# Turning k, q, v and the delta output by VectorE blocks and transfers instead of TensorE transposes

## The chip, the cores and the metric

The kernel runs on one core of a Trainium2 chip. The metric is the time of one execution on the device, in microseconds (us); the time of a kernel is the median of its runs. A core has TensorE (PE, matmuls; PEld is its loading of weights), VectorE (DVE), ScalarE (ACT), GpSimd (POOL) and SyncE (SP), which work side by side, each through its own instructions in order. SP and POOL, and now and then ACT, issue the transfers (DMAs) between DRAM and the core's memory.

## The reference, cut to what matters

One layer of a decoder with 512 new tokens of a prompt (`x_prompt`) and 8 single tokens (`x_sample`). All data are float32.

```python
xn = rmsnorm(h, norm_mix)
proj = xn @ w_in                        # 2048 -> q | k | v | z (1024 each) | beta, decay (8 each) | pool (1024)
qkv_c, new_conv = short_conv(conv_buf, proj[..., :3072], conv_w)    # 4 taps over the tokens, then SiLU
q = l2norm(q) * (128 ** -0.5); k = l2norm(k)                        # 8 heads of 128
# per chunk of tokens, with the cumulated gates g and beta b:
m  = strictly_lower(b * (k @ k.T) * decay)        # then (I + m) is inverted
qk = lower((q @ k.T) * decay)
v_new = u - w @ S
o  = (q * exp(g)) @ S + qk @ v_new
S  = S * exp(g_last) + (k * exp(g_last - g)).T @ v_new
dn_out = rmsnorm(o, dn_norm) * silu(z)
h = h + concat(dn_out, pool_out) @ w_out
h = h + swiglu(rmsnorm(h, norm_ffn)); y = rmsnorm(h, norm_final)
```

## The kernel before, in words

Activations lie with their features on the 128 partitions and the 520 tokens (8 samples, 512 of the prompt) along the row. A projection tile of 128 columns is a `product`: 16 steps over the input features, each with three matmuls (high and low parts of both operands) for each of two halves of the tokens (`CHUNKS`). The weights come in granules of 128 x 1024: SP loads `raw` (L131), ScalarE rounds it to `hi` (L135), VectorE takes the rest as `lo` (L137), with three buffers of each.

The changed part runs from 40 to about 520 us. For each half of the heads (`b` = 0, 1; four heads) it does the four k tiles, then the four z tiles, then for each head a q tile and a v tile. `qkv_tile` ends with the four taps on VectorE (L737, L739) and SiLU on ScalarE (L740).

The smaller work of the delta rule is written as Python generators which `Weave` steps through: `product` calls `weave.step()` after each of its steps (16 times a product), and a task's `yield n` says how many steps it rests. There are two tracks, and each runs its tasks in the order in which they were added, a task not before its delay. TensorE's instructions run in just this order of the program. For the other engines and the DMA queues a planner (the Tile framework) orders the instructions by priority and by when it expects them to be ready; each engine then takes its own list in order. Loads and cuts of weights, and evictions, have a raised priority.

The tasks:
- `keys(h)`: K times K per chunk of 128 tokens (L766), the transposes of k's tile (L769), the sums of squares of the transposed tile by ScalarE (`squares`, L757), the factors `sck` on POOL and VectorE, `nn` (K times K with its factors and decay, L781) and `kd` (k with tokens on partitions, times a factor, L783). The diagonal 32 x 32 blocks of `nn` go to DRAM (`nd_d`, L788).
- `eliminate(b)`: inverts all the diagonal blocks of four heads on VectorE (L807, L809), and sends the results to DRAM (`ud_d`, L810, L813), from where `qv_tiles` loads them into `utf` (L1093).
- `delta(h, qT, vT)`: `nn` with the inverse blocks (L831), the transposes of q (L838) and their squares, three rounds (`it`) that widen the inverse (L850 on TensorE, L852 on VectorE), with K times Q (L857) and `aq` (L860) in the first and the transposes of v (L865) and `vs` (L867) in the second, then four chunks of the recurrence (L877 to L896) with R, W and S passing between TensorE, VectorE and ScalarE, and last the norm of the output (`on`, L910).
- `gate(h, on)`: 8 steps later, the transposes of `on` (L916), and one VectorE instruction that multiplies them into `mix[h]` (L918).

`d1tile(tag, ...)` gives a buffer of the pool by its tag, of which there are `BUFS[tag]`. `pst()` gives one of five PSUM banks. Later stages (w_out, the gate and up projections, the down projection) are Strassen products with the queue of POOL carrying the intermediate (`a_d`, `st`, L1776).

Of the kernel before, what the change touches and what calls it, by code (L numbers as in the profile page):

```python
# [8 lines left out]
F32 = mybir.dt.float32  # L9
# [3 lines left out]
ALU = mybir.AluOpType  # L13
# [22 lines left out]
    "ext": 2, "y": 1, "ys": 1, "g3": 3, "junk": 1, "ss": 2, "rr": 2, "nb": 1, "u": 1, "tm": 2, "xt_": 1, "uu": 2,  # L36
    "qts": 1, "fq": 2, "aq": 1, "vs": 1, "R": 2, "W": 2, "S": 2, "so": 2, "ro": 2, "s0": 2, "s2": 1, "kd": 4, "st": 2,
}
# [31 lines left out]
def decoder_kernel(ctx, tc, x_prompt, x_sample, state_delta, state_conv, state_pool, norm_mix, w_in,  # L70
# [450 lines left out]
    with ExitStack() as p1:  # L521
# [208 lines left out]
        def qkv_tile(sec, h, out, ext=None):  # L730
# [10 lines left out]
            pool.tensor_copy(ccp[:, :, t], ext[:, SEQ:SEQ + 3])  # L741

        def decay(h):

            gcb = d1tile("g3", [P, SEQ], "gcb")
            sp.dma_start(gcb, gcr_d[h:h + 1, :].broadcast_to([P, SEQ]))
            dm = d1tile("g3", [P, SEQ], "dm")
            for c in range(NCH):
                dve.scalar_tensor_tensor(dm[:, ck(c)], gcb[:, ck(c)], gcs[:, c, h:h + 1], mneg,
                                         op0=ALU.subtract, op1=ALU.min)  # L750
            act.activation(dm, dm, AF.Exp)
            return gcb, dm
# [7 lines left out]
        def keys(h):  # L760
            kT, nn = mixb[:, h % 4, 0:SEQ], mixb[:, 4 + h % 4, 0:SEQ]
            kd = kds[h] = d1tile("kd", [P, SEQ], "kd")
            _, dm = decay(h)
            gp_ = pst()
            for c in range(NCH):
                te.matmul(gp_[:, ck(c)], kT[:, ck(c)], kT[:, ck(c)], start=True, stop=True)  # L766
            ktp = pst()
            for c in range(NCH):
                te.transpose(ktp[:, ck(c)], kT[:, ck(c)], ident)  # L769
            ss = d1tile("ss", [P, NCH], "ss")  # L770
            squares(ktp, ss)
            dve.tensor_scalar(ss, ss, EPS, None, op0=ALU.add)
# [7 lines left out]
            for c in range(NCH):  # L780
                dve.scalar_tensor_tensor(nn[:, ck(c)], gp_[:, ck(c)], fk[:, c:c + 1], dm[:, ck(c)],  # L781
                                         op0=ALU.mult, op1=ALU.mult)
            dve.tensor_tensor(v3(kd), v3(ktp), bc3(ad), op=ALU.mult)  # L783
            yield 6 if h < 3 else 2
# [31 lines left out]

        def delta(h, qT, vT):
            kT, nn, kd = mixb[:, h % 4, 0:SEQ], mixb[:, 4 + h % 4, 0:SEQ], kds[h]
# [16 lines left out]
            pool.tensor_copy(v3(cur), udf)  # L835
            qtp = pst()
            for c in range(NCH):
                te.transpose(qtp[:, ck(c)], qT[:, ck(c)], ident)  # L838
            ss = d1tile("ss", [P, NCH], "ss")
            squares(qtp, ss)  # L840
            dve.tensor_scalar(ss, ss, EPS, None, op0=ALU.add)
            fq = d1tile("fq", [P, NCH], "fq")
            pow_mhalf(fq, ss)
            dve.tensor_scalar(fq, fq, float(P) ** -0.5, None, op0=ALU.mult)
            yield 2
            for it in range(3):
                yp = v3(pst())
                j = slice(32 * it + 32, P)
                for c in range(NCH):
# [3 lines left out]
                                         op0=ALU.mult, op1=ALU.add)  # L853
                if it == 0:
                    gq_ = pst()
                    for c in range(NCH):
                        te.matmul(gq_[:, ck(c)], kT[:, ck(c)], qT[:, ck(c)], start=True, stop=True)  # L857
                    aq = d1tile("aq", [P, SEQ], "aq")
                    for c in range(NCH):
                        dve.scalar_tensor_tensor(aq[:, ck(c)], gq_[:, ck(c)], fk[:, c:c + 1], dm[:, ck(c)],  # L860
                                                 op0=ALU.mult, op1=ALU.mult)
                if it == 1:
                    vtp = pst()
                    for c in range(NCH):
                        te.transpose(vtp[:, ck(c)], vT[:, ck(c)], ident)  # L865
                    vs = d1tile("vs", [P, SEQ], "vs")
                    dve.tensor_tensor(v3(vs), v3(vtp), bc3(ik), op=ALU.mult)  # L867
                yield 2
# [3 lines left out]
            for c in range(NCH):  # L872
# [24 lines left out]
                S = S2  # L897
                yield 1
            sp.dma_start(nd_prompt[0, 0, h], S)

# [9 lines left out]
            dve.tensor_tensor(v3(on), v3(op_), bc3(ro), op=ALU.mult)  # L910
            weave.add(gate(h, on), 1, 8)

        def gate(h, on):
            otp = pst()
            for c in range(NCH):
                te.transpose(otp[:, ck(c)], on[:, ck(c)], ident)  # L916
            yield 1
            dve.scalar_tensor_tensor(mix[h][:, NB:NTOK], otp, dnw, mix[h][:, NB:NTOK], op0=ALU.mult, op1=ALU.mult)  # L918

# [169 lines left out]
        def qv_tiles(h):  # L1089
            utf = utfs[h % 2].rearrange("p a c j -> p (a c) j")  # L1090
            for q in range(4):
                r = slice(32 * q, 32 * q + 32)
                sp.dma_start(utf[r, :, r], ud_d[h, q].rearrange("a c s j -> s (a c) j"))  # L1093
            qT = d1tile("s0", [P, SEQ], "qT")
            qkv_tile(0, h, qT)
            vT = d1tile("s2", [P, SEQ], "vT")
            qkv_tile(2, h, vT)
            weave.add(delta(h, qT, vT), 0, 1)

        kds = {}  # L1100
        for b in range(2):
            for h in range(4 * b, 4 * b + 4):
                qkv_tile(1, h, mixb[:, h % 4, 0:SEQ],
                         {0: ext_first, 1: ext_second}.get(h))
                if h == 0:
                    weave.add(states())
                    weave.add(gates(), 1)
                weave.add(keys(h), 1, 16)
            weave.add(eliminate(b), 1)
# [967 lines left out]
```

## Time and profile before

| | |
|---|---|
| median of 3 runs | 2161.36 us (2161.24 to 2161.99) |
| span of the profiled execution | 2158.9 us |
| TensorE busy | 2136.1 us |
| VectorE busy | 1746.4 us |
| ScalarE busy | 929.6 us |
| POOL busy | 433.8 us |
| moved by DMA | 297.04 MB |

The times given are those of the unprofiled runs. The profiled execution has a span from its first to its last instruction; that is shorter than a run's time by what lies around it (2161.36 - 2158.9 = 2.5 us here).

How such lines are read: a group reads "line engine operation out<-in shape xcount | busy us, mean ns of one | idle before us <-who ended it". A line of a timeline reads "start us, us, engine line operation out<-in xcount [idle before <-releaser]", where several like instructions may be merged into one line. A wait reads "engine line waited for <- releaser: us in all, times, longest". A window reads "from:to length, busy (xinstructions) of PE, PEld, DVE, ACT, POOL, then the TensorE clock granted (1.00 is full), the mean share of the 16 DMA engines in use, GB/s". An instruction's summary gives its duration as min/median/max in ns and the first and last start. A line of the queues gives packets, MB and share of the 16 engines' span.

### The profile page before, as it was taken

The page shows a single profiled execution, that of the slowest core. Times are in us where ns is not written, and L with a number is a line of the kernel's source. Part 1 is how long each engine was busy: PE and PEld are TensorE (multiplying, and loading weights), DVE is VectorE, ACT ScalarE, POOL GpSimd, SP SyncE. Part 2 cuts the span into 40 slices and gives each one's busy share as a digit, 9 for nine tenths or more (in the row PEclk, how much of TensorE's full clock was granted, in tenths as well). Part 3 has the DMA queues.
Part 4 walks back from the last instruction along what each step waited for, and adds up shares of the span by engine and source line. Part 5 has one row for each costly group of instructions (what it writes and reads, how often), then busy time and mean ns, then how long its engine had stood idle before and what let it go on. Part 6 is the DMA issues. An engine that isn't in the chain of part 4 may idle for free.

```text
span 2158.9 us, 42980 instructions
## 1 busy us (share of the span) xinstructions
PE 2136.1 (99%) x17809; PEld 2128.8 (99%) x17809; DVE 1746.4 (81%) x2619; ACT 929.6 (43%) x1404; POOL 433.8 (20%) x512
## 2 busy tenths in 40 slices
PE   8999999999999999999999999999999999999998
PEld 7999999999999999999999999999999999999998
DVE  7786667666499979988988888888877898887997
ACT  6533443432264545434433434434334444435444
POOL 2210110111012202233233233232113302003100
PEclk9999999999999999999999999999999999999999
DMA  8343234323445543554554454454446746438343
GB/s 281 92 110 91 76 94 112 88 76 96 120 121 161 152 119 111 155 166 141 145 166 139 147 167 143 142 163 134 125 147 189 234 111 205 115 103 247 93 108 119
DMA packets 442497, 297.04 MB, mean 138 GB/s; under 512 B 26556, under 2 KB 423253, under 8 KB 438957
## 3 DMA queue, kind: packets, MB, share of 16 engines
q1 hardware_dynamic: 422733, 219.94, 36.3%
q0 software_dynamic: 18256, 73.55, 10.5%
q8 instruction: 139, 2.28, 0.5%
q10 hardware_dynamic: 1312, 0.80, 0.1%
q14 instruction: 57, 0.47, 0.1%
HBM read 251.47 MB, written 43.43 MB: 137 GB/s over the span
## 4 chain that ended last, share of the span: by engine, by line
PE 86%; DVE 8%; DMA 2%; issue 2%; ACT 1%; POOL 1%; SPq 0%; DVEq 0%; POOLq 0%; ACTq 0%
PE dn L1223 20%; PE dn L1222 20%; PE dn L1224 20%; PE mm L168 6%; PE mm L170 6%; PE mm L169 6%; DVE lo L1216 2%; DVE raw L1244 1%; PE dn L850 1%; DMA st<-a_d 1%; DVE lo L137 1%; POOL st L1776 0%; DMA xt<-in_x_prompt_dram 0%; PE dn L960 0%; PE dn L857 0%
## 5 line engine op out<-in xcount | busy, mean ns | idle before, releaser
L1215 ACT CAST hi<-raw 128x1024 fp32r<-128x1024 f32 (+1 forms) x422 | 427.4, 1027 | 400.2 <-DVE raw L1244 206.5
L1216 DVE TENSOR_TENSOR lo<-raw,hi 128x1024 fp32r<-128x1024 f32 (+1 forms) x422 | 527.4, 1270 | 87.1 <-ACT hi L1215 85.6
L168 PE MATMUL mm<-xh,hi 128*128 128x256 f32 (+1 forms) x1280 | 379.7, 297 | 2.4 <-DVE mixa L259 2.4
L169 PE MATMUL mm<-xl,hi 128*128 128x256 f32 (+1 forms) x1280 | 361.5, 282 | 0.9 <-DVE xl L350 0.7
L170 PE MATMUL mm<-xh,lo 128*128 128x256 f32 (+1 forms) x1280 | 361.8, 283 | 0.4 <-DVE lo L137 0.4
L168 PEld LDWEIGHTS mm<-xh,hi 128*128 128x128 f32 x1280 | 241.4, 189 | 3.7 <-DVE mixa L259 3.1
L169 PEld LDWEIGHTS mm<-xl,hi 128*128 128x128 f32 x1280 | 241.7, 189 | 1.7 <-DVE xl L350 1.7
L170 PEld LDWEIGHTS mm<-xh,lo 128*128 128x128 f32 x1280 | 240.8, 188 | 0.6 <-DVE lo L137 0.6
L1244 DVE TENSOR_TENSOR raw<-raw 128x1024 f32<-128x1024 f32 (+1 forms) x130 | 175.3, 1349 | 2.2
L1223 PE MATMUL dn<-b21l,hi 128*128 128x260 f32 x620 | 175.7, 283 | 0.4 <-DVE b21l L1786 0.4
L1224 PE MATMUL dn<-b21h,lo 128*128 128x260 f32 x620 | 175.4, 283 | 0.0
L1222 PE MATMUL dn<-b21h,hi 128*128 128x260 f32 x620 | 175.0, 282 | 0.0
L1224 PE MATMUL dn<-b11h,lo 128*128 128x260 f32 x612 | 173.4, 283 | 1.2 <-DVE lo L1216 1.1
L1223 PE MATMUL dn<-b11l,hi 128*128 128x260 f32 x612 | 173.3, 283 | 0.0
L1222 PE MATMUL dn<-b11h,hi 128*128 128x260 f32 x612 | 172.7, 282 | 0.0
L1222 PE MATMUL dn<-T1h,hi 128*128 128x260 f32 x556 | 158.1, 284 | 0.0
L1223 PE MATMUL dn<-T1l,hi 128*128 128x260 f32 x556 | 157.7, 284 | 0.0
L1224 PE MATMUL dn<-T1h,lo 128*128 128x260 f32 x556 | 156.7, 282 | 0.0
L1222 PE MATMUL dn<-B22h,hi 128*128 128x260 f32 x548 | 155.9, 284 | 0.0
L1223 PE MATMUL dn<-B22l,hi 128*128 128x260 f32 x548 | 155.6, 284 | 0.0
L1224 PE MATMUL dn<-B22h,lo 128*128 128x260 f32 x548 | 154.6, 282 | 0.4 <-DVE lo L1216 0.4
L135 ACT CAST hi<-raw 128x1024 fp32r<-128x1024 f32 (+2 forms) x86 | 87.1, 1014 | 148.2 <-PE mm L169 139.4
(659 smaller groups left out, 6422.5 us busy)
## 6 DMA issues: line engine op xcount, KB each, us to landing
raw<-in_w_gate_up_dram SPq DMA_DIRECT2D x134, 512.0 KB
raw<-in_w_in_dram SPq DMA_DIRECT2D x79, 512.0 KB
a_d<-mixa POOLq DMA_DIRECT2D x22, 1040.0 KB, 5.5
raw<-in_w_down_dram SPq DMA_DIRECT2D x48, 448.0 KB
mixb<-in_w_gate_up_dram SPq DMA_DIRECT2D x41, 512.0 KB
raw<-in_w_out_dram SPq DMA_DIRECT2D x25, 512.0 KB
st<-a_d POOLq DMA_DIRECT2D x49, 260.0 KB, 6.5
raw<-in_w_down_dram SPq DMA_DIRECT2D x24, 512.0 KB
```

What stands on the lines that cost most here:

```text
L135: act.copy(hi[:, r], raw[:, r])
L137: dve.tensor_tensor(lo[:, r], raw[:, r], hi[:, r].bitcast(F32), op=ALU.subtract)
L168: te.matmul(acc[ci], wh, hi[k][:, c0:c1], start=(k == 0), stop=False)
L169: te.matmul(acc[ci], wh, lo[k][:, c0:c1], start=False, stop=False)
L170: te.matmul(acc[ci], wl, hi[k][:, c0:c1], start=False, stop=(k == len(w) - 1))
L850: te.matmul(yp[0:96, c, j], xt_[:, c, :], udf[:, c, j] if it == 0 else v3(cur)[:, c, j], start=True, stop=True)
L1215: act.copy(hi, raw)
L1216: dve.tensor_tensor(lo, raw, hi.bitcast(F32), op=ALU.subtract)
L1222: te.matmul(acc, wh[:, k, :], xf[:, k, :], start=start and k == 0, stop=False)
L1223: te.matmul(acc, wh[:, k, :], xg[:, k, :], start=False, stop=False)
L1224: te.matmul(acc, wl[:, k, :], xf[:, k, :], start=False, stop=stop and k == wh.shape[1] - 1)
L1244: dve.tensor_tensor(r[name], r[a], r[b], op=op)
```

## The change

A helper turns a 128 x 512 tile in blocks. VectorE transposes each 32 x 32 block in its place into a buffer `bt`. SP writes `bt` to DRAM, and four reads, one for each group of 32 partitions, bring the blocks back into their transposed places, in runs of 32 elements (128 B). It stands for the four groups of TensorE transposes: of k (straight after its tile, into `kds[h]`), of v (after its tile, in place), of q (into `qk`) and of the output `on` (in place; the gate now follows after 12 steps).

With it, k's sums of squares are read from the diagonal of K times K by VectorE, four instructions with `ident` and an accumulating output. `kd`'s factor is multiplied in the first round of `delta`, `vs`'s in the second as before, and K times Q moves from the first round to the third. The squares of q are taken from the turned tile after the second chunk. In `qv_tiles` v's tile comes before q's. There are more buffers (`vs`, `bt`, `tq`), and the memory set aside for descriptors of POOL's transfers (`dynamic_dma_scratch_size`) is set to 8192.

```diff
-    "qts": 1, "fq": 2, "aq": 1, "vs": 1, "R": 2, ...
+    "qts": 1, "fq": 2, "aq": 1, "vs": 2, "bt": 2, "tq": 1, "R": 2, ...
...
+        tok_d = dram.tile([4, H, NCH, P, P], F32, name="tok_d")
+
+        def turn_blocks(kind, h, src, dst):
+
+            bt = d1tile("bt", [P, SEQ], "bt")
+            dve.transpose(bt, src)
+            d = tok_d[kind, h]
+            sp.dma_start(d.rearrange("c p f -> p c f"), v3(bt))
+            rows = d.rearrange("c (i p) (j q) -> j p (c i) q", p=32, q=32)
+            for j in range(4):
+                sp.dma_start(dst[32 * j:32 * j + 32, :].rearrange("p (n q) -> p n q", q=32), rows[j])
...
         def keys(h):
-            kd = kds[h] = d1tile("kd", [P, SEQ], "kd")
...
-            ktp = pst()
+            ss = d1tile("ss", [P, NCH], "ss")
+            junk = d1tile("junk", [P, P], "junk")
             for c in range(NCH):
-                te.transpose(ktp[:, ck(c)], kT[:, ck(c)], ident)
-            ss = d1tile("ss", [P, NCH], "ss")
-            squares(ktp, ss)
+                dve.scalar_tensor_tensor(junk, gp_[:, ck(c)], 1.0, ident, op0=ALU.mult, op1=ALU.mult,
+                                         accum_out=ss[:, c:c + 1])
...
-            dve.tensor_tensor(v3(kd), v3(ktp), bc3(ad), op=ALU.mult)
...
-        def delta(h, qT, vT):
+        def delta(h, qT, qk, vs):
...
-            qtp = pst()
-            for c in range(NCH):
-                te.transpose(qtp[:, ck(c)], qT[:, ck(c)], ident)
-            ss = d1tile("ss", [P, NCH], "ss")
-            squares(qtp, ss)
-            dve.tensor_scalar(ss, ss, EPS, None, op0=ALU.add)
-            fq = d1tile("fq", [P, NCH], "fq")
-            pow_mhalf(fq, ss)
-            dve.tensor_scalar(fq, fq, float(P) ** -0.5, None, op0=ALU.mult)
...
                 if it == 0:
+                    dve.tensor_tensor(v3(kd), v3(kd), bc3(sck[:, h, 2, :]), op=ALU.mult)
+                if it == 2:
                     gq_ = pst()
...
                 if it == 1:
-                    vtp = pst()
-                    for c in range(NCH):
-                        te.transpose(vtp[:, ck(c)], vT[:, ck(c)], ident)
-                    vs = d1tile("vs", [P, SEQ], "vs")
-                    dve.tensor_tensor(v3(vs), v3(vtp), bc3(ik), op=ALU.mult)
+                    dve.tensor_tensor(v3(vs), v3(vs), bc3(ik), op=ALU.mult)
...
                 S = S2
                 yield 1
+                if c == 1:
+                    ss = d1tile("ss", [P, NCH], "ss")
+                    squares(qk, ss)
+                    dve.tensor_scalar(ss, ss, EPS, None, op0=ALU.add)
+                    fq = d1tile("fq", [P, NCH], "fq")
+                    pow_mhalf(fq, ss)
+                    dve.tensor_scalar(fq, fq, float(P) ** -0.5, None, op0=ALU.mult)
...
-            weave.add(gate(h, on), 1, 8)
+            turn_blocks(3, h, on, on)
+            weave.add(gate(h, on), 1, 12)

         def gate(h, on):
-            otp = pst()
-            for c in range(NCH):
-                te.transpose(otp[:, ck(c)], on[:, ck(c)], ident)
+            dve.scalar_tensor_tensor(mix[h][:, NB:NTOK], on, dnw, mix[h][:, NB:NTOK], op0=ALU.mult, op1=ALU.mult)
             yield 1
-            dve.scalar_tensor_tensor(mix[h][:, NB:NTOK], otp, dnw, mix[h][:, NB:NTOK], op0=ALU.mult, op1=ALU.mult)
...
+            vs = d1tile("vs", [P, SEQ], "vs")
+            qkv_tile(2, h, vs)
+            turn_blocks(2, h, vs, vs)
             qT = d1tile("s0", [P, SEQ], "qT")
             qkv_tile(0, h, qT)
-            vT = d1tile("s2", [P, SEQ], "vT")
-            qkv_tile(2, h, vT)
-            weave.add(delta(h, qT, vT), 0, 1)
+            qk = d1tile("tq", [P, SEQ], "qk")
+            turn_blocks(0, h, qT, qk)
+            weave.add(delta(h, qT, qk, vs), 0, 1)
...
+                kds[h] = d1tile("kd", [P, SEQ], "kd")
+                turn_blocks(1, h, mixb[:, h % 4, 0:SEQ], kds[h])
                 weave.add(keys(h), 1, 16)
...
-    nc = _bacc.Bacc("TRN2", target_bir_lowering=False, num_devices=1)
+    nc = _bacc.Bacc("TRN2", target_bir_lowering=False, num_devices=1, dynamic_dma_scratch_size=8192)
```

More of the change, by code (lines that the diff above doesn't have):

```diff
@@ L36 @@
     "ext": 2, "y": 1, "ys": 1, "g3": 3, "junk": 1, "ss": 2, "rr": 2, "nb": 1, "u": 1, "tm": 2, "xt_": 1, "uu": 2,
-    "qts": 1, "fq": 2, "aq": 1, "vs": 1, "R": 2, "W": 2, "S": 2, "so": 2, "ro": 2, "s0": 2, "s2": 1, "kd": 4, "st": 2,
+    "qts": 1, "fq": 2, "aq": 1, "vs": 2, "bt": 2, "tq": 1, "R": 2, "W": 2, "S": 2, "so": 2, "ro": 2, "s0": 2, "s2": 1, "kd": 4, "st": 2,
 }
```

## The prediction

> **What bounds the kernel now.** I read the page first for its busy shares, then the waits of TensorE between 40 and 540 us (the stretch in which the changed heads run), then the windows by stage.
>
> ```profile
> span 2158.9 us, 42980 instructions
> ...
> PE 2136.1 (99%) x17809; PEld 2128.8 (99%) x17809; DVE 1746.4 (81%) x2619; ACT 929.6 (43%) x1404; POOL 433.8 (20%) x512
> ...
> PE mm L168 <- DVE mixa L259: 2.4, 3, 1.1
> ...
> 118.00:148.00 30.00, 28.48 (x236) 28.06 (x235) 27.84 (x73) 6.72 (x9) 0.00 (x0) 1.00 0.33 90
> 160.00:192.00 32.00, 32.00 (x281) 32.00 (x280) 19.27 (x44) 12.79 (x30) 3.23 (x8) 1.00 0.37 96
> 192.00:224.00 32.00, 32.00 (x281) 32.00 (x281) 20.27 (x46) 13.29 (x32) 3.04 (x8) 1.00 0.30 80
> ```
>
> The first two lines: TensorE is busy for 99% of the span. The third: in the changed stretch it waits 2.4 us in all, for VectorE, which is 93% busy (27.84 of 30 us) while it inverts the diagonal blocks. The last two are one head of q and v products each: TensorE 32.00 of 32, VectorE about 20, the DMA engines 0.30 to 0.37. So the kernel is bound by the order of TensorE's instructions, which is fixed by the program. An instruction taken out there shortens the end by the room that it held, as long as nothing new makes TensorE wait. After 640 us the change touches nothing on TensorE, and what is won before is kept.
>
> **What is removed.** Four kinds of turns, 32 transposes each.
>
> ```profile
> L769 PE MATMUL dn<-ident,mixb x32: 272/273/273, 83.0 to 328.4; 128*128 128x128 f32 x32
> L838 PE MATMUL dn<-ident,qT x32: 272/272/273, 162.8 to 485.1; 128*128 128x128 f32 x32
> L865 PE MATMUL dn<-ident,vT x32: 272/273/281, 168.3 to 491.3; 128*128 128x128 f32 x32
> L916 PE MATMUL dn<-ident,mixb x32: 270/272/273, 198.0 to 518.3; 128*128 128x128 f32 x32
> ...
> 162.76 0.60 PE L838 MATMUL dn<-ident,qT 128*128 128x128 f32 x4
> 163.12 0.37 PE L168 MATMUL mm<-xh,hi 128*128 128x264 f32 x1
> ...
> 163.56 0.28 PE L168 MATMUL mm<-xh,hi 128*128 128x256 f32 x1
> 164.28 0.28 PE L168 MATMUL mm<-xh,hi 128*128 128x256 f32 x1
> ...
> 168.34 0.61 PE L865 MATMUL dn<-ident,vT 128*128 128x128 f32 x4
> ...
> 197.97 0.60 PE L916 MATMUL dn<-ident,mixb 128*128 128x128 f32 x4
> 198.32 0.38 PE L168 MATMUL mm<-xh,hi 128*128 128x264 f32 x1
> ```
>
> Matmuls overlap, so their durations are not what one saves; starts are. The four transposes of q start at 162.76 and the next matmul at 163.12: 0.36 us. Those of the gate: 198.32 - 197.97 = 0.35. The change of mode around a group (0.37 for the first matmul after it, not 0.28) stays, since other full-precision matmuls of the same task stand beside each group. 128 transposes are 32 groups: 32 x 0.36 = **11.5 us** off TensorE. (The two L168 rows 0.72 apart are one step of the weave, six matmuls; I use it below.) Also gone from ScalarE are the 32 squares of the turned k; ScalarE is not the bound, and I count nothing for it.
>
> [...]
>
> **What is added on VectorE.** Durations, from the groups between 40 and 540 us:
>
> ```profile
> L737 DVE TENSOR_SCALAR y<-ext,prm 128x512 f32<-128x512 f32 x24 | 12.9, 536 | 0.5
> L739 DVE SCALAR_TENSOR_TENSOR y<-ext,prm,y 128x512 f32<-128x512 f32 x72 | 53.9, 748 | 1.2
> L781 DVE SCALAR_TENSOR_TENSOR mixb<-dn,sck,dm 128x128 f32<-128x128 f32 x32 | 9.0, 342 | 0.0
> L783 DVE TENSOR_TENSOR kd<-dn,sck 128x512 f32<-128x512 f32 x8 | 5.4, 681 | 0.0
> L812 DVE COPY ut<-u 64x1024 f32<-64x1024 f32 x2 | 2.2, 1122 | 0.1
> ```
>
> No VectorE transpose is in the trace. Below it is bounded by L737 (0.54 us for 512 elements), above by the whole of L812 (1.12); I take half of L812, a copy that permutes as many elements, 0.56. K's squares from K times K's diagonal are four instructions like L781: 4 x 0.28 = 1.1 us a head. kd's multiplication (0.68) moves from the keys into the delta task; v's and the gate's stay where they were.
> - A q and v head gets three transposes and kd's product, 3 x 0.56 + 0.68 = 2.4 us: VectorE goes from 20 to some 22.5 of 31 us. Hidden by TensorE's own work.
> - Before the first elimination four heads of keys add 4 x (1.1 + 0.56 - 0.68) = 4 us. The inversion may start by that much later. After it come the loads of its blocks (the row at 153.55 below, whose last issue ends at 156.10 and lands up to 2.84 us later, at 158.9) and the first delta task at 161.90. That leaves 3.0 us, less the 4 x 0.36 = 1.4 us that TensorE itself comes earlier: 1.6. So this costs between 0 and 2.4 us, once (the second time, 382.37 against 388, there is room); I take 0.5.
>
> **What is added on SP and in DMAs.** Each turn is one 256 KB write and four 64 KB reads in 128 B runs, and the reads wait for the write. 32 turns are 160 issues.
>
> ```profile
> 153.55 2.55 SPq L1093 DMA_DIRECT2D utf<-ud_d  x5
> ...
> 370.78 0.52 SPq L813 DMA_DIRECT2D ud_d<-ut  x1
> ...
> 374.80 1.81 SPq L1093 DMA_DIRECT2D utf<-ud_d  x4
> ...
> 321.57 1.76 SPq L788 DMA_DIRECT2D nd_d<-mixb  x4
> ...
> 324.48 0.20 POOL L791 MEMSET mixb<- 32x128 f32 x1 [0.26 <-DMA nd_d<-mixb]
> ...
> 377.52 2.01 SPq L1093 DMA_DIRECT2D utf<-ud_d  x4
> ...
> 382.37 0.61 POOL L835 COPY uu<-utf 128x512 f32<-128x512 f32 x1 [2.61 <-DMA utf<-ud_d]
> ...
> 321.50:325.00 3.50, 3.50 (x32) 3.50 (x31) 1.86 (x7) 2.47 (x4) 0.79 (x4) 1.00 0.12 19
> ...
> q1 hardware_dynamic: 422733, 219.94, 36.3%
> ```
>
> A 256 KB write is read back 374.80 - 370.78 = 4.0 us after its issue. Four issues of 128 B runs take 1.8 us. After the last of them nd_d's data land in 324.48 - (321.57 + 1.76) = 1.15 us, utf's in 382.37 - (377.52 + 2.01) = 2.84. A round trip is so 4.0 + 1.8 + 1.15 to 2.84 = **7.0 to 8.7 us** if SP is free. Load: nd_d's four writes are 512 runs of 128 B in 0.12 x 3.5 us x 16 engines = 6.7 us, 13 ns each; a larger packet of SP's queue takes 0.363 x 2158.9 x 16 / 422733 = 30 ns. A turn is 512 x 30 + 2048 x 13 ns = 42 us over 16 engines, 2.6 us; three in a head of 31 us raise the DMA share from 0.3 to some 0.55. No bound.
>
> Now each turn's lead, from the first head:
>
> ```profile
> 161.90 1.03 PE L831 MATMUL dn<-utf,mixb 128*128 128x96 f32 x8
> ...
> 166.48 0.63 ACT L740 ACTIVATE vT<-y 128x512 f32<-128x512 f32 x1
> ...
> 177.88 0.39 PE L896 MATMUL dn<-W,aq 128*128 128x128 f32 x2
> ...
> 192.29 0.69 DVE L910 TENSOR_TENSOR mixb<-dn,ro 128x512 f32<-128x512 f32 x1
> ...
> 193.62 1.02 PE L831 MATMUL dn<-utf,mixb 128*128 128x96 f32 x8
> ```
>
> A head takes 193.62 - 161.90 = 31.7 us, a product half, 15.9. A product's SiLU ends 167.11 - 161.90 = 5.2 us after its last matmul, so a turned tile lands 5.2 + 0.56 + 7.0 to 8.7 = 12.8 to 14.5 us after it.
> - v, now first, is used one product and 6.4 us later (168.34 - 161.90): at 22.3. Eight us in hand.
> - q's squares come after the second chunk, 177.88 - 161.90 = 16.0: 1.5 to 3.2 us in hand. ScalarE waits there if it is late, and behind it the copies of W that TensorE needs.
> - K times Q moves two rounds later. TensorE reaches it two steps behind the place of v's old transposes, less q's old transposes: 6.4 + 1.4 - 0.4 = 7.4 us after the product. The q tile is there at 5.2; VectorE's extra work eats about one us of the 2.2 between.
> - k is used tens of us later.
> - The gate: the output is ready at 192.98, lands at 192.98 + 0.56 + 7.0 to 8.7 = 200.5 to 202.2. Its VectorE instruction comes 12 steps on, where the old transposes came after 8 at 197.97: 197.97 + 4 x 0.72 = 200.9 at the earliest. VectorE so waits 0 to 1.3 us; behind it are the next delta's L852 and the cuts of weights, for which TensorE has two steps, 1.4 us. I count 0.5 us in all.
>
> The sum against the profiled execution: 2158.9 - 11.5 + 0.5 + 0.5 = 2148.4. The median, 2161.36, lies 2.5 us above that span, so **2150.9 us**. Without any new wait it is 2149.9, and 2147.5 if the 2.4 us for L259 go too.
>
> The smaller descriptor scratch bears on POOL's transfers, later on:
>
> ```profile
> 1952.49 4.94 POOL L1776 DMA_DIRECT2D st<-a_d  x7 [112.51 <-PE dn L1224]
> ...
> SPq L131 <- DVE lo L137: 205.7, 48, 18.5
> ...
> DVE dm L749 <- DMA gcb<-gcr_d: 2.2, 1, 2.2
> ...
> DVE tm L807 <- DMA nb<-nd_d: 1.6, 2, 1.3
> ```
>
> Seven loads in a run are issued at 0.71 us each, so none waits for room; with half the room I expect the same.
>
> **The rivals.**
> 1. *VectorE waits for transfers that SP holds up; slower.* SP takes its queue in order, and weight loads stand in it until a buffer is cut free: 205.7 us in 48 waits, 4.3 each (the row above). If the gate's write or reads stand behind one such wait, the tile lands at 201.35 + 4.3 = 205.7, VectorE stands for 4.8 us from 200.9, and TensorE, with 1.4 in hand, loses 3.4 a head, 27 us in all: 2150 + 27 = **2177**. It decides from 1.44 us lost a head (11.5 / 8), a hold of 2.8. For it: one queue, five more issues a turn, and one VectorE that evicts and cuts too. Against: VectorE waited for DMAs only 2.2 + 1.6 us in this stretch before (the last two rows).
> 2. *The same in part; no change.* If every second head is caught by it, 4 x 3.4 = 13.6 us cancel the 11.5: **2163**.
> 3. *Durations count, not starts:* 2161.4 - 34.8 = **2127**. The starts speak against it.
> 4. *Short runs are slow.* If nd_d's landing is all run time (128 runs, 8 an engine, in 1.15 us, 0.144 each), a turn's 2048 runs, 128 an engine, take 18 us, some 15 more than counted, and eight gates wait that long: 2150 + 8 x (15 - 1.4) = **2259**. The 13 ns a run from the DMA share speak against it. [...]
> 5. *Half the scratch makes POOL's loads wait:* up to one landing for each, a few us on the chain near 1960; slower at worst, **2170**.
>
> **How the numbers follow.** Forecast 0.66; rival 1 0.14, rival 2 0.16, rival 3 0.01, rivals 4 and 5 together 0.03. Within 0.2%, about what a measurement can tell from no change, is 2157.0 to 2165.7. Faster 0.67, same 0.16, slower 0.17. The range goes from 2147.5 to 2172: below lie rival 3 and a little of the forecast, above the worse half of rival 1 and rival 4, less than 0.2 together. The forecast's own range is 2147.5 to 2156.
>
> **What would show it.** TensorE's instructions fall by 128 to 17681, and a head's period shrinks from 31.7 to 31.7 - 3 x 0.36 = 30.6 us with TensorE still busy throughout. TensorE's waits before 540 us should stay under 4 us, and VectorE's on the turned tiles near zero. Wrong would be: waits of VectorE on the gate's tile or of ScalarE on q's turned tile by microseconds a head, TensorE waiting for L852, L259 or lo, or SP's reads standing long behind L131.

## The result: slower, and the profile after

| | before | after |
|---|---|---|
| median | 2161.3 us (2161.09 to 2161.99) | 2201.31 us (2199.07 to 2202.61) |
| span of the profiled execution | 2158.9 us | 2200.9 us |
| ratio of the times, 95% interval | | 1.0184 (1.0169 to 1.0198) |

The change makes the kernel 40 us slower. From the page of after, the busy shares, and TensorE's busy tenths and granted clock by slices of 55 us:

```profile
PE 2132.7 (97%) x17681; PEld 2124.2 (97%) x17681; DVE 1770.4 (80%) x2715; ACT 922.3 (42%) x1342; POOL 441.9 (20%) x512
...
PE   8986999699999999999999999999999999999998
...
PEclk9997999899999999999999999999999999999999
```

The 128 transposes are gone (17681 instructions against 17809), and yet TensorE's busy share fell: two slices have holes, the fourth and the eighth, and the clock is lower there too. TensorE's waits between 36 and 660 us (engine, line that waited, releaser: us in all, times, longest) name the holes; here the longest four:

```profile
PE dn L841 <- DMA utf<-ud_d: 38.4, 2, 21.7
PE dn L964 <- DMA s<-in_state_delta_dram: 3.7, 1, 3.7
PE dn L851 <- DVE uu L853: 2.3, 3, 1.0
PE mm L168 <- DVE ccs L259: 2.1, 1, 2.1
```

Twice, once for each half of the heads, the first delta task (L841) waits for `utf`, the inverted diagonal blocks; 38.4 us in both. The blocks were late because the elimination began late. Its load `nb`, in the summary of that tile's transfers (before, then after; the first and the last start stand behind the durations):

```profile
L797 SPq DMA_DIRECT2D nb<-nd_d x2: 483/505/527, 114.5 to 336.7; - x2
```

```profile
L807 SPq DMA_DIRECT2D nb<-nd_d x2: 483/505/527, 137.0 to 374.3; - x2
```

22.5 us late the first time, and 37.6 the second, of which 21.7 are the first wait. The timelines of SP's queue show where that starts: `gcr_d` (the cumulated gates on their way through DRAM) and the first load of `gcb` (its broadcast, which the keys of a head need), before, then after:

```profile
80.09 0.30 SPq L621 DMA_DIRECT2D gcr_d<-gr  x1
82.27 0.82 SPq L746 DMA_DIRECT2D gcb<-gcr_d  x2
```

```profile
85.53 0.39 SPq L131 DMA_DIRECT2D raw<-in_w_in_dram  x1
85.97 0.47 SPq L621 DMA_DIRECT2D gcr_d<-gr  x1
86.53 2.00 SPq L753 DMA_DIRECT2D kd<-tok_d  x4
95.76 0.39 SPq L131 DMA_DIRECT2D raw<-in_w_in_dram  x1
96.19 0.58 SPq L758 DMA_DIRECT2D gcb<-gcr_d  x1
```

The reads of the turned k stand in SP's list ahead of `gcb`, and with them a weight load. From 88.53 (86.53 + 2.00) to 95.76 SP issues nothing: the load waits for a buffer, which is cut free by VectorE's `lo` L137:

```profile
89.58 0.69 DVE L856 TENSOR_TENSOR kd<-kd,sck 128x512 f32<-128x512 f32 x1
...
94.52 1.22 DVE L137 TENSOR_TENSOR lo<-raw,hi 128x1024 fp32r<-128x1024 f32 x1
```

`lo` ends at 95.74, and only then do the weight load and the small load behind it go out, `gcb` 13.9 us late (96.19 against 82.27); the transfers of three more heads follow behind further weight loads. In VectorE's list the squares and `kd`'s product (which the planner put here, into the keys' stage, not into the delta task) stand ahead of that `lo`, but they don't make it late. In the kernel before, the same cut and the same weight load (the fifteenth of `raw`) come 1.2 us later still:

```profile
95.74 1.22 DVE L137 TENSOR_TENSOR lo<-raw,hi 128x1024 fp32r<-128x1024 f32 x1
...
96.98 0.40 SPq L131 DMA_DIRECT2D raw<-in_w_in_dram  x1
```

So what differs is the place in SP's list: before, the first `gcb` goes out ahead of the fourteenth and fifteenth weight load, after the change behind both, and it inherits their waits for a buffer. The reads of the turn themselves take 2 us.

The clock adds to a wait. Windows at the first hole (length, TensorE's busy time and instructions, granted clock, DMA share, GB/s):

```profile
160.00:164.00 4.00, 0.68 (x6) 1.00 0.57 122
164.00:168.00 4.00, 0.00 (x0) 0.57 0.41 108
...
184.00:186.00 2.00, 2.00 (x11) 0.50 0.21 32
186.00:188.00 2.00, 2.00 (x14) 0.50 0.00 0
188.00:190.00 2.00, 2.00 (x18) 0.89 0.13 21
```

TensorE has worked 0.68 us of the first window, so it stops at 160.7. A mean of 0.57 in the second means full clock for 0.56 us of it: the clock falls to 0.50 at 164.6, 3.9 us after the stop. It is full again at 188.4 (0.89 in the last row), 6.1 us after TensorE resumed at 182.3 (160.7 + 21.67). The matmuls of L169 and L170 start 0.21 us apart at 0.50 (185.06 and 185.27) and 0.12 us at 1.00 (188.75 and 188.87), so the 6.1 us lose 6.1 x 0.09 / 0.21 = 2.6 us more. Three other waits are followed by work at 0.50: the 2.1 us for VectorE's `ccs` (until 147.1) by 3.4 us of it, the second wait for `utf` by 3.3, the wait for s0 by 6.8. Together TensorE works 19.6 us at 0.50, which loses 8.4.

So the sum: TensorE is idle for 624 - 576.10 = 47.9 us between 36 and 660 us, against 624 - 620.21 = 3.8 before:

```profile
36.00:660.00 624.00, 576.10 (x4788) 571.29 (x4788) 418.23 (x1035) 220.20 (x402) 76.41 (x149) 0.96 0.49 122
```

```profile
36.00:660.00 624.00, 620.21 (x5261) 616.66 (x5261) 435.70 (x996) 251.19 (x498) 77.23 (x161) 1.00 0.39 106
```

44.1 us more of idleness and 8.4 of low clock behind the waits, less the 11.5 that the prediction counts for the removed transposes: 41.0 us. The span grew by 42.0.

### The profile page after: what moved, and what is told of

The parts are those of the page before. It is cut to its first block, busy times and chain, and to the rows that moved or that the text cites. A ratio compares the mean times of both kernels' runs of the same rounds, so it can differ in the third digit from the quotient of the medians.

```text
span 2200.9 us, 43027 instructions
## 1 busy us (share of the span) xinstructions
PE 2132.7 (97%) x17681; PEld 2124.2 (97%) x17681; DVE 1770.4 (80%) x2715; ACT 922.3 (42%) x1342; POOL 441.9 (20%) x512
## 2 busy tenths in 40 slices
DMA packets 526978, 313.84 MB, mean 143 GB/s; under 512 B 94652, under 2 KB 507733, under 8 KB 523437
## 4 chain that ended last, share of the span: by engine, by line
PE 82%; DVE 11%; DMA 3%; issue 2%; ACT 2%; SPq 0%; POOL 0%; DVEq 0%; ACTq 0%; POOLq 0%
PE dn L1232 21%; PE dn L1231 21%; PE dn L1233 21%; PE mm L168 5%; PE mm L169 4%; PE mm L170 4%; DVE lo L137 1%; DVE lo L1225 1%; DVE u L819 1%; DVE tm L817 1%; DVE y L739 1%; PE dn L851 1%; DMA raw<-in_w_in_dram 1%; DVE raw L1253 0%; DMA nb<-nd_d 0%
## 5 line engine op out<-in xcount | busy, mean ns | idle before, releaser
L169 PE MATMUL mm<-xl,hi 128*128 128x256 f32 (+1 forms) x1280 | 363.5, 284 | 0.9 <-DVE xl L350 0.5
L170 PE MATMUL mm<-xh,lo 128*128 128x256 f32 (+1 forms) x1280 | 363.4, 284 | 0.4 <-DVE lo L137 0.4
L169 PEld LDWEIGHTS mm<-xl,hi 128*128 128x128 f32 x1280 | 244.0, 191 | 1.7 <-DVE xl L350 1.7
L170 PEld LDWEIGHTS mm<-xh,lo 128*128 128x128 f32 x1280 | 242.7, 190 | 0.6 <-DVE lo L137 0.6
L1417 POOL TENSOR_TENSOR mixa<-mixa 128x520 f32<-128x520 f32 x22 | 51.2, 2328 | 496.3 <-DVE mixa L1411 496.3
```

Of the source, the lines that this page charges most:

```text
L169: te.matmul(acc[ci], wh, lo[k][:, c0:c1], start=False, stop=False)
L170: te.matmul(acc[ci], wl, hi[k][:, c0:c1], start=False, stop=(k == len(w) - 1))
L1417: pool.tensor_tensor(q[:, 4:8:2, :], q[:, 1:4:2, :], q[:, 0:2, :], op=ALU.subtract)
```

## The experiments

Theory Q: SP's one queue, in order; the turns stand ahead of the elimination's small transfers. Rival D: VectorE is late by the squares and blocks. Rival T: the added transfers slow all others. All ratios are to before, with 95% intervals.

### Which part: k on TensorE, squares on ScalarE, k later, the scratch

```diff
 # e1: k turned by TensorE for kd, the squares stay with the diagonal; v, q, output by transfers
-                turn_blocks(1, h, mixb[:, h % 4, 0:SEQ], kds[h])
...
+            for c in range(NCH):
+                te.transpose(ktp[:, ck(c)], kT[:, ck(c)], ident)
...
+            dve.tensor_tensor(v3(kd), v3(ktp), bc3(ad), op=ALU.mult)
 # e2: squares from TensorE's turn, on ScalarE; k's transfers stay
-                dve.scalar_tensor_tensor(junk, gp_[:, ck(c)], 1.0, ident, ..., accum_out=ss[:, c:c + 1])
...
+                te.transpose(ktp[:, ck(c)], kT[:, ck(c)], ident)
+            squares(ktp, ss)
 # e3: k's turn after z_tile(h), four tiles later
                 z_tile(h)
+                turn_blocks(1, h, mixb[:, h % 4, 0:SEQ], kds[h])
 # e4: before, with dynamic_dma_scratch_size=8192
```

> The changed kernel with only the transfer turn of k undone: k is turned by TensorE as before (for kd alone), its squares still come from K times K's diagonal on VectorE, and v, q and the output are turned by transfers. Theory Q (the order of SP's queue: k's writes and reads, with weight loads that wait for a buffer between them, hold up the gcb loads and the nd_d stores, so the elimination starts 22 us late and TensorE waits 21.7 and 16.7 us for utf): the waits for utf fall under 3 us in all, nb is loaded within 5 us of its time before (114.5), the time is 2150 to 2161. Rival D (VectorE: K's squares there hold up the keys): the waits stay above 25 us, time above 2190.

> The changed kernel with only K's squares undone: k is transposed by TensorE a second time, for ScalarE's squares alone; kd still comes by transfers. Theory Q: the waits for utf stay above 25 us, nb still comes about 20 us late, time 2195 to 2208. Rival D: the waits vanish, time 2150 to 2161.

> The changed kernel with k's turns written behind the z tiles instead of behind the k tiles, which lowers their priority for the planner; nothing else differs. In SP's list the first gcb load now stands 31st, not 47th. Theory Q: nb comes 10 to 20 us sooner than in the changed kernel, the waits for utf fall to less than half (under 19 us), time 2150 to 2178. Rival D: no difference, 2195 to 2205.

> The kernel before with only the descriptor scratch set to 8192. Theories Q and D: no difference, 2160 to 2163. Rival S (the smaller scratch makes POOL's transfers wait): more than 4 us slower, 2166 and up.

| | time, us | ratio | wait for utf, us | nb issued at |
|---|---|---|---|---|
| e1, k on TensorE | 2167.32 | 1.0031 (1.0018 to 1.0043) | none | 118.2, 336.4 |
| e2, squares on ScalarE | 2190.91 | 1.0138 (1.0122 to 1.0153) | 25.6 | 133.2, 366.0 |
| e3, k later | 2173.05 | 1.0057 (1.0042 to 1.0072) | 5.5 | 116.3, 343.8 |
| e4, scratch | 2161.09 | 0.9999 (0.9990 to 1.0008) | none | 114.1, 336.7 |

Without k's transfers (e1), or with them later (e3), `nb` is nearly in time, with the squares on VectorE. Without the squares (e2) it is still 19 us late, though the time lies 4 us below what Q expected. So k's transfers hold up the elimination, and the squares' part of the wait is the smaller one, 12.8 of the 38.4 us. The scratch does nothing. But e1 and e3 stay above before, against the expectation for e1: something else costs some 6 us.

### The order in SP's queue

```diff
 # e5: the whole change; e6: the same edit on e1; e11: on e3, gcr_d as well
+            with tc.high_priority(offset=AHEAD):     # the same for nd_d, nb, ud_d, utf, s0
                 sp.dma_start(gcb, gcr_d[h:h + 1, :].broadcast_to([P, SEQ]))
```

> The whole change, with the loads of gcb, nb, utf and s0 and the writes of nd_d and ud_d placed by the planner at the same high priority as the weight loads, so that SP issues them ahead of the reads of the turns. Theory Q (the elimination starts late because its transfers stand in SP's queue behind the reads of the turned k, and those behind weight loads that wait for a buffer): the wait for utf falls from 38.4 us to under 6, the wait for s0 (3.7 us) goes, nb is issued within 6 us of its time before (114.5 and 336.7 us), and with the lower clock after the waits gone too the time comes to 2155 to 2168 us. Theory T (the added transfers slow every transfer, or VectorE is simply late with the squares and blocks): the order of the queue changes little, utf is still waited for by 20 us or more, 2185 to 2201 us.

> k turned on TensorE again (for the decayed keys only, the squares stay with the diagonal), and the same transfers at high priority. Beside the kernel with k on TensorE and no priority (2167.3 us) this tells what the s0 wait of 3.8 us and the half clock of some 7 us behind it are worth: if they are what keeps that kernel 6 us above before, 2155 to 2161 us here; if it is the many small waits for VectorE in the delta rounds (5.5 us in sum), 2164 to 2169 us.

> The whole change with k's turns in the tiles of z (alone: 2173.1 us) and high priority for the gcr_d, gcb, nd_d, nb, ud_d, utf and s0 transfers (alone, without gcr_d: 2173.8 us). If both remedies address the same cause, the queue ahead of the elimination, together they bring nb within 4 us of before and the waits for utf and s0 to nothing, and the time to 2155 to 2163 us, with the small waits for VectorE in the delta rounds (4 to 8 us) left. If the remainder is not the queue, it stays at 2168 to 2174 us.

e5 took 2173.78 us, 1.0059 (1.0044 to 1.0074): 27.5 of the 40 us come back from the order of SP's list alone, with every byte and every VectorE instruction of the change in place. Its transfers of `nb` and TensorE's waits:

```profile
L810 SPq DMA_DIRECT2D nb<-nd_d x2: 482/510/537, 122.1 to 343.9; - x2
```

```profile
PE dn L846 <- DMA utf<-ud_d: 8.2, 1, 8.2
```

That misses what Q expected (at most 2168 us, under 6 us of waiting, `nb` within 6 us), but is far from T's 20 us of waiting and more. TensorE waits 7.5 us for `uu` too, a wait that stayed untraced. e6 missed: 2180.35 us, 1.0088 (1.0073 to 1.0103), worse than e1 without the priorities; TensorE waits 7.8 us for `vs` and 7.5 for `uu`. e11 missed too: 2175.15 us, 1.0067 (1.0054 to 1.0080), though its first `nb` goes out at 114.9. Waits and SP's queue in e11:

```profile
PE dn L889 <- DVE vs L872: 10.6, 2, 8.4
...
PE dn L847 <- DMA utf<-ud_d: 0.5, 1, 0.5
```

```profile
154.67 0.56 SPq L751 DMA_DIRECT2D tok_d<-bt  x1
157.45 4.40 SPq L1105 DMA_DIRECT2D utf<-ud_d  x9
...
167.18 0.57 SPq L754 DMA_DIRECT2D vs<-tok_d  x1
...
172.24 1.10 SPq L754 DMA_DIRECT2D vs<-tok_d  x2
```

`utf` is all but in time, but its loads and two weight loads now stand ahead of the reads of v's turn, whose issues end 18.7 us after that of its write (173.34 - 154.67; with SP free it was to be 5.8). The wait has moved from `utf` to `vs`. The queue was put in another order, and then another transfer was late.

### Single turns, and the order of v and q

```diff
 # e7: before, only the output turned by transfers.  e9: e7 with s0's loads at high priority
-            for c in range(NCH):
-                te.transpose(otp[:, ck(c)], on[:, ck(c)], ident)
+            turn_blocks(3, h, on, on)
 # e10: e9 and q turned by transfers, q's tile first as before; v and k on TensorE
             qkv_tile(0, h, qT)
+            turn_blocks(0, h, qT, qk)
 # e12: e1 with s0's loads at high priority.  e15: e12 with k's squares on ScalarE as before
 # e16: e10 with k's squares from the diagonal
 # e8: before, only in another order: v's tile ahead of q's, K times Q in the third round
-                if it == 0:
+                if it == 2:
                     gq_ = pst()
```

> The kernel before with only the delta output turned by VectorE blocks and transfers (scratch of 8192 for the memory of the blocks). 32 transposes less on TensorE, 2.9 us at 0.09 us each. If a turn whose result nobody waits for is free, 2157.5 to 2160 us; if its five transfers push the utf and s0 loads and the weights back in SP's queue, 2161 to 2168 us.

> The kernel that turns only the delta output (2165.5 us), with the s0 loads at high priority in SP's queue. In it the turn of head 6's output and a store stood ahead of an s0 load (526.6 us against 523.3 us before) and TensorE waited 3.8 us, then ran at a lower clock. If that one wait and its clock are the whole loss, 2157.5 to 2159.5 us (2.9 us below before, the 32 transposes). If the turns cost by something else (transfers, VectorE), it stays at 2161 us or above.

> The kernel with k on TensorE and v, q and output by transfers (2167.3 us), with the s0 loads alone at high priority. If the s0 wait (3.8 us) and the half clock behind it are its loss, 2159 to 2162 us; if the small waits for VectorE in the rounds, 2164 us and above.

e7 took 2165.46 us, 1.0022 (1.0012 to 1.0031): the one turn whose result nobody waits for still cost 4 us. SP's queue in before and in e7, and TensorE's timeline in e7:

```profile
523.31 0.37 SPq L957 DMA_DIRECT2D s<-in_state_delta_dram  x1
```

```profile
516.12 0.37 SPq L750 DMA_DIRECT2D tok_d<-bt  x1
518.45 2.21 SPq L753 DMA_DIRECT2D mixb<-tok_d  x4
525.51 0.39 SPq L131 DMA_DIRECT2D raw<-in_w_in_dram  x1
525.95 0.55 SPq L1022 DMA_DIRECT2D out_dram<-st  x1
526.59 11.56 SPq L967 DMA_DIRECT2D s<-in_state_delta_dram  x3
```

```profile
530.90 0.59 PE L970 MATMUL dn<-kqs,s 128*128 128x2 f32 x2 [3.80 <-DMA s<-in_state_delta_dram]
```

The s0 load of the samples goes out 3.3 us later, and TensorE waits 3.80 us; then it runs at a clock of 0.50 for 5.7 us. Here too the order differs and not the weight load, which isn't late (525.51, against 525.96 in before): in before s0 goes out ahead of it, in e7 behind it. With that load ahead the time falls by 5.9 us in both kernels: e9 2159.61 us, 0.9995 (0.9986 to 1.0004), from 2165.46; e12 2161.42, 1.0002 (0.9993 to 1.0011), from 2167.32. So this wait of 3.8 us cost 5.9. e12 is where it was expected, e9 a tenth above its range: the s0 wait was e1's 6 us.

> The output and q turned by transfers, k and v on TensorE as before, q's tile first as before, s0 loads at high priority. q's turn has the whole tile of v (some 17 us) to arrive in. 64 transposes less, 5.8 us by starts: if each turn is free where its result has time, 2154.5 to 2157.5 us; if q's transfers take a place in SP's queue that the utf or gcb loads need, 2159 to 2166 us.

> v, q and the output by transfers with v's tile first, k wholly as before (turned by TensorE, squares on ACT), s0 at high priority: the kernel of 2161.4 us without the diagonal squares. With the kernel of q and output (2153.3 us) and the next one it is a square of two parts: v's turn and order, and the diagonal squares. If the diagonal squares on VectorE are what is late in the rounds, 2150 to 2156 us here; if it is v's turn and the late K times Q, 2158 to 2162 us.

> q and output by transfers, v on TensorE, as in the kernel of 2153.3 us, with k's squares from the diagonal on VectorE (k still turned on TensorE for the decayed keys). If the diagonal squares lengthen the way to the elimination by 4 us, as in the kernel of 2161.4 us (nb at 118.3 us against 114.7 us), and that has cover before the first wait for utf: within 2 us of 2153.3 us. If they cost, 2157 to 2162 us.

| | time, us | ratio | by transfers | squares of k |
|---|---|---|---|---|
| e10 | 2153.32 | 0.9966 (0.9953 to 0.9979) | q, output | ScalarE |
| e16 | 2154.36 | 0.9974 (0.9964 to 0.9983) | q, output | VectorE |
| e15 | 2158.29 | 0.9987 (0.9978 to 0.9997) | v, q, output | ScalarE |
| e12 | 2161.42 | 1.0002 (0.9993 to 1.0011) | v, q, output | VectorE |

e10 beats both kernels, by 7.8 us against before, where 5.8 were expected; it lies 1.2 us below its range. The two turns don't bring the same, though each takes away 32 transposes: the output's alone brought 1.5 us (e9), q's 6.3 more. In e9 TensorE waits 1.6 us for `uu`, in e10 not; the rest of the difference was not traced. e10's longest wait in that stretch is that of before:

```profile
PE mm L168 <- DVE mixa L259: 2.4, 3, 1.3
```

The diagonal squares cost 1 to 3 us. v's turn with its order costs 5.0 us (e15 against e10) where 32 transposes less should have brought 2.9. In e15 TensorE waits for the rounds of VectorE:

```profile
PE dn L853 <- DVE uu L855: 3.0, 4, 1.2
```

> The kernel before, only in the order of after: the tile of v ahead of that of q, and K times Q in the third round in place of the first. No work is removed or added. If the order costs nothing by itself: within 1.5 us of 2161.3 us. If the later K times Q makes the delta rounds wait for VectorE (aq is then needed two rounds sooner after its product), 2163 to 2168 us, and this is a part of the 6 us that stay in the kernel with k on TensorE.

e8 missed both ways: 2197.33 us, 1.0166 (1.0149 to 1.0183), for an order that adds no work. The waits of TensorE, then the windows behind the first of them and the whole stretch:

```profile
PE dn L838 <- ACT qT L740: 24.6, 8, 3.8
```

```profile
166.00:168.00 2.00, 2.00 (x14) 0.69 0.06 15
168.00:170.00 2.00, 2.00 (x13) 0.50 0.00 0
170.00:172.00 2.00, 2.00 (x21) 0.96 0.21 33
...
36.00:660.00 624.00, 595.92 (x4961) 591.03 (x4960) 403.09 (x946) 229.91 (x468) 68.29 (x149) 0.98 0.35 96
```

With q's tile last, the old transposes of q at the head of the delta task wait for its SiLU in each of the eight heads, 3.1 us on average. The first is followed by 3.4 us of half clock (the rows' means put it from 166.8 to 170.2). Over the whole stretch the mean clock is 0.98, where before has 1.00: some 624 x 0.02 / 0.5 = 25 us at 0.50, an estimate from that mean, which by the starts above lose about 25 x 0.09 / 0.21 = 11. With the 24.6 of waiting that is some 35 us, and 36 were measured. So e8 prices an order that the change itself doesn't have, since it takes q's squares away from there. The later K times Q makes TensorE wait by no more than 0.4 us in all here (`uu`); but the stop ahead of each delta task gives VectorE time that it hasn't in the change, so what K times Q costs there stays open.

### The turns on another queue

```diff
 # e13: the whole change, the turns on POOL.  e14: the same with act.dma_start
-            sp.dma_start(d.rearrange("c p f -> p c f"), v3(bt))
+            pool.dma_start(d.rearrange("c p f -> p c f"), v3(bt))
...
-                sp.dma_start(dst[32 * j:32 * j + 32, :].rearrange("p (n q) -> p n q", q=32), rows[j])
+                pool.dma_start(dst[32 * j:32 * j + 32, :].rearrange("p (n q) -> p n q", q=32), rows[j])
 # e17: the same two lines on e15.  e18: e13 with the elimination's two VectorE lines at high priority
```

> The whole change, with the five transfers of every turn issued by POOL in place of SP; all other orders as the planner puts them. Theory Q (the place in SP's one queue is the cause, not the added bytes and not VectorE): nb is issued within 5 us of before (114.5 and 336.7 us), the waits for utf and s0 fall to under 3 us, and the time is 2152 to 2165 us. Theory T (the added 128-byte runs slow what else is carried): the loads of SP stay late wherever the turns are issued, 2185 us and above. A third outcome, POOL's own work (rr, the copies of u) late behind its waiting reads: TensorE waits for uu or utf's copy, and 2165 to 2185 us.

> The same with the five transfers issued by ACT, which has more work of its own behind them than POOL. Theory Q: nb within 5 us of before, no long wait for utf or s0; but each turn's first read holds ACT some 2.5 us until the write has landed, and the weights' first halves (hi) are ACT's: if that is covered, 2152 to 2165 us, if not, TensorE waits for hi or the converted tiles, 2165 to 2190 us. Theory T: as on SP, 2185 us and above.

e13 took 2160.40 us, 0.9995 (0.9986 to 1.0005): 41 us come back, with none of SP's priorities changed. Its `nb`, and TensorE's waits:

```profile
L807 SPq DMA_DIRECT2D nb<-nd_d x2: 483/510/537, 119.6 to 342.9; - x2
```

```profile
PE dn L841 <- DMA utf<-ud_d: 4.0, 1, 4.0
```

The time fits Q; the wait is 4 us in place of one under 3, and `nb` is 5.1 and 6.2 us late in place of 5 at most. Yet it isn't clean: issued by POOL, the same bytes go in fewer packets (the page's counts, after, then e13):

```profile
DMA packets 526978, 313.84 MB, mean 143 GB/s; under 512 B 94652, under 2 KB 507733, under 8 KB 523437
```

```profile
DMA packets 449154, 313.84 MB, mean 145 GB/s; under 512 B 29116, under 2 KB 425813, under 8 KB 445613
```

e14 is the cleaner case: between 36 and 660 us the share of the DMA engines in use is 0.49 at 121 GB/s, in after 0.49 at 122 and in e13 0.50 at 133 (into how many packets its transfers went was not shown). It took 2206.57 us, 1.0210 (1.0195 to 1.0225), outside what Q expected; the time alone would speak for T, and the waits don't (TensorE's, then ScalarE's):

```profile
PE dn L888 <- ACT W L885: 27.7, 12, 6.5
...
PE dn L841 <- DMA utf<-ud_d: 4.4, 1, 4.4
```

```profile
ACT W L885 <- DMA mixb<-tok_d: 11.5, 3, 4.1
```

`utf` is waited for by 4.4 us, not 38.4. The first `nb` is issued at 121.5; the second, at 364.3, comes 27.6 us later than in before, but TensorE itself has stood idle for 26.7 us more by then. Now ScalarE stands before reads whose write hasn't landed, and its copies of W stand behind. The wait goes where the queue is. So T falls: with the same DMA share and rate the wait for `utf` is all but gone (4.4 of 38.4 us) as soon as SP's list is free of the turns. Here the choice of the issuing engine decides over 46 us (2206.57 - 2160.40), by what stands behind a waiting transfer on it: in e14 TensorE waits 27.7 us for W, in e13 for nothing longer than 4.0.

> v, q and the output by transfers issued by POOL, k wholly as before (TensorE turns it, ACT squares it). On SP this kernel took 2158.3 us, with waits for uu and R of 3.8 us that the whole change on POOL's queue doesn't have. 96 transposes less, 8.6 us by starts. If those waits come from SP's queue too (VectorE's scaling of v waits for v's reads, and what stands behind it with it): 2150 to 2154 us, level with or below the kernel of q and output (2153.3 us). If they come from the later K times Q or the order of v and q: 2157 to 2160 us.

> The whole change with the turns on POOL's queue (2160.4 us), with the elimination's steps on VectorE at high priority. There nb came 5 us late and the elimination took 35.7 us (119.6 to 155.3 us), since the filter's taps of v stand between its steps, and TensorE waited 4.0 us for utf and ran at a lower clock. If VectorE's order is what is left of the loss: the elimination takes under 32 us, the wait for utf goes, 2151 to 2157 us. If the taps that now come later make v late: the wait moves to v, R or the tap's own readers, 2159 to 2166 us.

e17 took 2156.99 us, 0.9981 (0.9972 to 0.9990), between the two ranges: the waits for `uu` fall from 3.0 to 0.2 us, so those were SP's queue too, and a wait for S of 2.1 us takes their place. e18 took 2161.50 us, 0.9997 (0.9988 to 1.0006). The elimination takes 35.1 us (119.3 to 154.4) and the wait is still there:

```profile
PE dn L842 <- DMA utf<-ud_d: 5.1, 1, 5.1
```

But this doesn't test the theory, since the raised priority hardly moved VectorE's list: the taps still stand between the last steps (e13, then e18):

```profile
150.90 0.28 DVE L817 TENSOR_TENSOR tm<-nb,u 64x135 f32<-64x135 f32 x1
151.11 0.73 DVE L739 SCALAR_TENSOR_TENSOR y<-ext,prm,y 128x512 f32<-128x512 f32 x1
```

```profile
150.39 0.29 DVE L820 TENSOR_TENSOR u<-u,tm 64x135 f32<-64x135 f32 x1
150.60 0.74 DVE L739 SCALAR_TENSOR_TENSOR y<-ext,prm,y 128x512 f32<-128x512 f32 x1
```

From the first step to the last it takes 31.6 us in e13 and 31.5 in e18, against 27.8 in before; the steps themselves take 20.6 or 20.7 in all three. So of the 8.7 us by which the last step ends later in e13 than in before (155.2 against 146.4), 3.8 are other work between the steps, and 4.9 are the start: `nb` comes some 5 us late. In e16 and e1, which have the squares on VectorE too, it goes out at 118.0 and 118.2; in e15 and e10, with the squares on ScalarE, at 114.0 and 114.7, which puts most of that start down to the squares.

## Why the prediction was wrong

- **The step that failed** is the elimination: "The inversion may start by that much later", 4 us by VectorE's instructions, and a cost of "between 0 and 2.4 us, once". The 4 us were right for VectorE (118.2 in e1). But the sum asked only what VectorE adds, and not what SP's list puts ahead of `gcb`, `nd_d` and `nb`: the issues were counted (160) and their traffic, and leads were worked out for the turned tiles alone. It measured 22.5 and 37.6 us later, 38.4 us of waiting, and low clock behind it. The order of that list alone was worth 27.5 us (e5), the queue of the turns 41 (e13).
- "k is used tens of us later" was true of TensorE's use and false as a reason to cost k's turn at nothing: a transfer that nobody waits for still has a place in the list, and others come to stand behind it. The same holds for the output's turn, behind which s0 came late (e7: 5.9 us). Both come under the mechanism of rival 1, which the prediction applied to the gate alone.
- **Rival 1** named the mechanism, SP in order with weight loads that wait for buffers, but put it at the gate's tile (rival 2 is the same at every second gate). There it hardly happened: VectorE waited 2.5 us for it, once. Its price came from 4.3 us, the mean wait of a weight load; here four heads of keys hung on such waits one behind the other, the first of 7.2 us. (By its own numbers it decides from a hold of 2.4 us, 200.9 + 1.4 + 1.44 - 201.35, not 2.8; VectorE's wait is 2.8.)
- `kd`'s product was to move into the delta task; the planner put it into the keys' stage (89.58 above).
- **What held:** TensorE loses 128 instructions, and by starts: e10's 64 transposes brought 7.8 us (4.5 to 10.2 by the interval), where 5.8 were forecast and the durations would give 64 x 0.272 = 17.4 (rival 3, whose 34.8 is 128 x 0.272); that it comes so near is in part luck, by its halves of 1.5 and 6.3. q's turned tile held ScalarE by 0.9 us, once; v's, on SP's queue as the change has it, held nobody in the profile of after. Traffic is no bound (rival 4): the DMA share rose from 0.39 to 0.49. The scratch does nothing (rival 5, e4). A VectorE transpose takes 0.71 us, not 0.56, 0.15 more for each; no experiment prices that.
- **The clock** was left out: it cost some 8.4 of the 40 us.

What stays open: of the 7.9 us between e15's forecast gain over e10 (2.9) and its loss (5.0), waits of 3.8 us are seen (`uu` and R), and POOL's queue gives back 1.3; the rest, the price of the later K times Q in it, and the 3.7 us by which e17 stays above e10, were not traced to one cause.

## What to carry to other kernels

Before a transfer is added, read the list of the queue that issues it: what stands behind it, what stands ahead that waits, and who needs what is behind; a transfer that nobody waits for wasn't free where it changed the order of the others (e7, 5.9 us). Ask whether the replacement of work that is taken off a full engine shares a queue with a chain that is itself just in time: here q and the output paid (2153.3 us against 2161.3), v with its order cost 5.0 us (e15 against e10) and k's turns 34.0 (after against e1). A higher priority in such a queue removed a wait (s0 in e9 and e12, 5.9 us each), or only moved it to the next transfer (e11, 10.6 us for `vs`). Another issuing engine helped where little that TensorE needed stood behind the waiting transfers (POOL, 41 us back in e13), and not where its copies of W did (ScalarE, 27.7 us in e14).

## What the runs showed of the hardware

Between 40 and 700 us the clock granted to TensorE was at 0.50 four times in after: for 3.4 us with the wait of 2.1 us for `ccs`, for 23.9 and 17.1 with those of 21.7 and 16.7 for `utf`, and for 6.8 with that of 3.7 for s0. In e7 it was at 0.50 for 6.8 us with the wait of 3.80 for s0. In before, whose longest wait there is 1.1 us, it was 1.00 throughout. The length of a wait alone doesn't tell: e16 has one of 2.2 us and e17 one of 2.1, and their windows between 36 and 660 us, of 60 to 100 us each, all show 1.00, while 3.4 us at 0.50 would make 0.98 of 100. What tells these waits from that for `ccs` was not shown. The price of a wait varied too: one of 3.8 us cost 5.9 (e9, e12), eight of 3.1 us cost 36 in all (e8).

At the same 313.84 MB the page of e13, with the turns issued by POOL, counts 29116 packets under 512 B, and that of after, with SP, 94652: 65536 fewer. The issue of each 64 KB read took 0.65 us of POOL (e13).
